# Summing over 16 ranks with identity matmuls on TensorE in place of trees on VectorE, in a two-block decoder layer pair

## The chip, the cores and the metric

One core of a Trainium2 chip runs the whole program; seven others are idle. The metric is device time in microseconds (us) of one execution.

## The reference

Two transformer blocks run one after the other on 512 tokens of width 1024. The change lies in the routing of the first block's expert layer, which reads, cut to what matters:

```python
def peer_layer(h, w_q, keys, u, v):
    q = (h @ w_q).reshape(B, S, 8, 2, 128)
    sc = jnp.einsum('bshpd,phnd->bshpn', q, keys)
    v1, i1 = lax.top_k(sc[..., 0, :], 16)
    v2, i2 = lax.top_k(sc[..., 1, :], 16)
    cand = (v1[..., :, None] + v2[..., None, :])       # 16 x 16 sums of each head
    cidx = (i1[..., :, None] * 128 + i2[..., None, :])
    best, pos = lax.top_k(cand, 16)
    idx = jnp.take_along_axis(cidx, pos, axis=-1)      # the two keys of each of the 16 best
    gates = jax.nn.softmax(best, axis=-1)
    # then act = gelu(u[idx] . h), out = sum(gates * act * v[idx])
```

Of the 256 candidates of a head only 50 can be among the best 16: rank r of the first half pairs with the first 16 // (r + 1) ranks of the second.

## The kernel before

The order on each engine is written out by hand (`manual_schedule`): an engine runs its instructions in the order in which the code issues them, and waits in place for what the next one needs. Generators that `yield` estimated microseconds are woven: `weave(main, fill, per)` lets `main` run to its next yield and then takes one step of `fill` for each `per` microseconds yielded.

The expert layer has these stages here, one after the other:

- Scoring: queries and key scores on TensorE, and the top 16 of each half on VectorE.
- Decode, `decode(tt)` for four tiles of 128 tokens. VectorE forms the 50 candidates of 8 heads (`cand`), takes their best 16 (`top16`: MAX8, MATCH_REPLACE8, FIND_INDEX8) and then turns each position `pos` into two keys. For that it compares the position with the first position of each of the 16 rows (`ge` against `row_at`), multiplies the 0/1 result by the steps between neighbouring ranks' keys (`step1`, `sum1`), and adds over the 16 ranks with a tree of four additions (L895). The row's length times 1024 rides in the same sum and is taken apart with integer operations (L898 to L904). The column in the row is then looked up the same way (L914 to L919). `turn_slots` and `keep` transpose the keys and gates of the tile before (three L942 matmuls, two ScalarE copies, four VectorE operations).
- The gate build, `gate_build`: 48 chunks, in each a comparison `hot` and a product `ohG` on VectorE, and 24 small bf16 matmuls on TensorE (L1004), evacuated by ScalarE (`gst`, L1006) and written to DRAM.
- The expert stream over 128 groups of rows of u and v.

The work woven into decode and gate build is `u_stream`. One column `a` is 24 matmuls of 128x384 (`ps_o`, L105 to L107) over a granule of u that ScalarE and GpSimd (for a < 26, `FC`) or VectorE (from 26) split into `whi` and `wlo`; a GELU (`act`, L729) ends it. A column of the first 40 is four steps of six matmuls. `early` holds the first 161 steps: decode takes one per yielded microsecond (`PER_B`), gate build one per 1.5 (`PER_C`), and what is left is issued after the gate build, before the expert stream's first v matmul (L105 to L107 with `wh`, `wl`).

Of the kernel before, what the change touches and what calls it, by code (L numbers as in the profile page):

```python
# [11 lines left out]
F32 = mybir.dt.float32  # L12
F32R = mybir.dt.float32r
BF = mybir.dt.bfloat16
I32 = mybir.dt.int32
U32 = mybir.dt.uint32
AF = mybir.ActivationFunctionType
OP = mybir.AluOpType
# [607 lines left out]
PH, PK, TOPK = 8, 128, 16  # L626
LENS = [TOPK // (i + 1) for i in range(TOPK)]
# [23 lines left out]
def top16(K, pool, work, n, tag):  # L651

    nc = K.nc
    rest = [pool.tile([128, n], F32, name="rest_" + tag, bufs=len(work)) for _ in work]
    for vals, idx, src in work:
        nc.vector.max(out=vals[:, 0:8], in_=src)
    for (vals, idx, src), r in zip(work, rest):
        nc.vector.match_replace(out=r, in_to_replace=vals[:, 0:8], in_values=src, imm_value=-3.0e38)
    for vals, idx, src in work:
        nc.vector.max_index(out=idx[:, 0:8], in_max=vals[:, 0:8], in_values=src)  # L660
    for (vals, idx, src), r in zip(work, rest):
        nc.vector.max(out=vals[:, 8:16], in_=r)
    for (vals, idx, src), r in zip(work, rest):
        nc.vector.max_index(out=idx[:, 8:16], in_max=vals[:, 8:16], in_values=r)


def peer(K, mh, w_out):
    with ExitStack() as ctx:
        ctx.enter_context(K.tc.manual_schedule())
        return peer_body(K, mh, w_out, ctx)  # L670


def peer_body(K, mh, w_out, ctx):
    nc, tc, A = K.nc, K.tc, K.A
    K.psum(ctx, mm=4, tp=2, o=2)
    P = ctx.enter_context(tc.tile_pool(name="peer", bufs=1))
    idx0 = P.tile([128, PH * TOPK], I32, name="idx0")
# [59 lines left out]
    h = mh  # L737
    with ExitStack() as c0:
        R = c0.enter_context(tc.tile_pool(name="h2", bufs=1, reuse_waits="tile"))
# [39 lines left out]
        for tt in (3, 0):  # L779
# [4 lines left out]
            for half in range(2):  # L784
                p = K.bank()
# [14 lines left out]
    with tc.tile_pool(name="route", bufs=1, reuse_waits="tile") as R:  # L800
        keys = K.xp.tile([128, 16, 128], F32, name="keys", tag="x1")
        nc.sync.dma_start(keys, A["peer_keys"])

        sh3, shk = [128, PH, TOPK], [128, TOPK, TOPK, PH]
        lens = R.tile([128, TOPK], F32, name="lens")
        row_at = R.tile(shk, BF, name="row_at")
        rank_at = R.tile(shk, BF, name="rank_at")
        for i in range(TOPK):
            nc.gpsimd.memset(row_at[:, i], float(OFFS[i]))
            nc.gpsimd.memset(lens[:, i:i + 1], 1024.0 * LENS[i - 1] if i else 0.0)  # L810
            nc.gpsimd.memset(rank_at[:, 8 * (i % 2) + 4 * (i // 2 % 2) + i // 4], float(i))
        If = R.tile([128, 2, PH, TOPK + 1], F32, name="If")
        nc.gpsimd.memset(If, 0.0)
        V = R.tile([128, NT, 2, PH, TOPK], F32, name="V")
# [10 lines left out]
        for c in range(NQ + 2):  # L825
            if c < NQ:
                pj[c] = K.proj_f(next(next_q), h)
            if 1 <= c <= NQ:
                p = K.bank("tp")
# [22 lines left out]
        RB = bctx.enter_context(tc.tile_pool(name="decode", bufs=1, reuse_waits="tile"))  # L852
        def decode(tt):

            nc.vector.tensor_copy(If[:, :, :, 1:], I[:, tt])
            v1, v2 = V[:, tt, 0], V[:, tt, 1]
            cand = RB.tile([128, PH, NCAND], F32, name="cand")
            for i in range(8):
                n = LENS[i]
                nc.vector.tensor_tensor(cand[:, :, OFFS[i]:OFFS[i] + n], v2[:, :, :n],  # L860
                                        v1[:, :, i:i + 1].to_broadcast([128, PH, n]), op=OP.add)
            nc.vector.tensor_tensor(cand[:, :, OFFS[8]:], v1[:, :, 8:],
                                    v2[:, :, 0:1].to_broadcast([128, PH, 8]), op=OP.add)
            yield 2.0
            best = RB.tile(sh3, F32, name="best")
            pos = RB.tile(sh3, U32, name="pos")
            for h0 in range(0, PH, 4):
                top16(K, RB, [(best[:, hh], pos[:, hh], cand[:, hh]) for hh in range(h0, h0 + 4)], NCAND, "c")
                yield 2.6
                if late and h0 == 0:  # L870
                    turn_slots()
                elif late:
                    keep()
                    yield 0.7

            e = RB.tile(sh3, F32, name="e")
            nc.vector.tensor_tensor(e, best, best[:, :, 0:1].to_broadcast(sh3), op=OP.subtract)
            kh = [128, TOPK, PH]
            at = RB.tile(kh, BF, name="at")
            nc.vector.tensor_copy(at, pos.rearrange("p h k -> p k h"))  # L880

            step1 = RB.tile(kh, F32, name="step1")
            nc.vector.tensor_tensor(step1, If[:, 0, :, 1:].rearrange("p h r -> p r h"),
                                    If[:, 0, :, :TOPK].rearrange("p h r -> p r h"), op=OP.subtract)
            nc.vector.tensor_tensor(step1, step1, lens[:, :, None].to_broadcast(kh), op=OP.add)
            ge = RB.tile(shk, BF, name="ge")
            nc.vector.tensor_tensor(ge, at[:, None].to_broadcast(shk), row_at, op=OP.is_ge)
            yield 2.2
            nc.scalar.activation(e, e, AF.Exp)
            sum1 = RB.tile(shk, F32, name="sum1")  # L890
            nc.vector.tensor_tensor(sum1, ge, step1[:, :, None].to_broadcast(shk), op=OP.mult)
            yield 2.2
            pk = sum1[:, 0]
            for n in (8, 4, 2, 1):
                nc.vector.tensor_tensor(sum1[:, :n], sum1[:, :n], sum1[:, n:2 * n], op=OP.add)  # L895
            yield 2.2
            pki = RB.tile(kh, I32, name="pki")
            nc.vector.tensor_copy(pki, pk)  # L898
            oi = RB.tile(kh, I32, name="oi")
            nc.vector.tensor_scalar(oi, pki, 10, None, op0=OP.arith_shift_right)  # L900
            nc.vector.tensor_scalar(pki, pki, 1023, None, op0=OP.bitwise_and)
            i1 = RB.tile(kh, F32, name="i1")
            i2 = RB.tile(kh, F32, name="i2")
            nc.vector.tensor_copy(i1, pki)  # L904
            nc.vector.tensor_tensor(at, at, oi, op=OP.subtract)
            yield 0.8

            step2 = RB.tile(kh, BF, name="step2")
            for d in range(2):
                def ranks(first):  # L910
                    return If[:, 1, :, first + d:first + d + TOPK - 1:2].rearrange("p h (q c) -> p h q c", c=2)
                nc.vector.tensor_tensor(step2[:, 8 * d:8 * d + 8].rearrange("p (c q) h -> p h q c", c=2),
                                        ranks(1), ranks(0), op=OP.subtract)
            nc.vector.tensor_tensor(ge, at[:, None].to_broadcast(shk), rank_at, op=OP.is_ge)  # L914
            yield 1.5
            nc.vector.tensor_tensor(ge, ge, step2[:, :, None].to_broadcast(shk), op=OP.mult)
            yield 1.1
            for n in (8, 4, 2, 1):
                nc.vector.tensor_tensor(ge[:, :n] if n > 1 else i2[:, None], ge[:, :n], ge[:, n:2 * n], op=OP.add)  # L919
            yield 1.3  # L920
            gs = RB.tile([128, PH], F32, name="gs")
            nc.vector.tensor_reduce(gs, e, axis=AX.X, op=OP.add)
            nc.vector.reciprocal(gs, gs)
            gt = gate0 if tt == 0 else RB.tile([128, PH * TOPK], F32, name="gt")
            g3 = gt.rearrange("p (k h) -> p h k", h=PH)
            nc.vector.tensor_tensor(g3, e, gs[:, :, None].to_broadcast(sh3), op=OP.mult)
            if tt == 0:
                nc.vector.scalar_tensor_tensor(idx0.rearrange("p (k h) -> p k h", h=PH), i1, float(PK), i2,
                                               op0=OP.mult, op1=OP.add)
                yield 1.0  # L930
                return
            yield 1.0
            late.append((i1, i2, gt, tt - 1))

# [2 lines left out]
        def turn_slots():  # L937

            i1, i2, gt, d = late.pop()
            p = K.bank("tp")  # L940
            for j, src in enumerate((i1.rearrange("p k h -> p (k h)"), i2.rearrange("p k h -> p (k h)"), gt)):
                nc.tensor.transpose(p[:, j * 128:(j + 1) * 128], src, K.ident)  # L942
            late.append((p[:, :384].rearrange("p (j c t) -> p c j t", j=3, t=OT), d))

# [12 lines left out]
        for tt in range(NT):  # L957
            weave(decode(tt), early, PER_B)
        turn_slots()
        keep()  # L960
        bctx.close()
# [115 lines left out]
    first = first_tile()  # L1077
# [18 lines left out]
    for a in range(-1, PK):  # L1096
        n = a + 1
# [852 lines left out]
```

## Time and profile before

| | us |
|---|---|
| median of three runs | 2105.06 (2104.98 to 2109.21) |
| the profiled execution | 2105.86 |
| its span, first to last instruction | 2103.60 |
| TensorE busy | 1985.4 (94%) |
| VectorE busy | 1596.6 (76%) |
| ScalarE busy | 891.1 (42%) |
| GpSimd busy | 479.2 (23%) |

A busy share is a mean over stages with different limits, so the stage around the change has to be looked at by itself. The 2.26 us between the span and the execution's time lie outside the instructions.

### The profile page before, as it was taken

How to read it: one execution, taken by the hardware profiler on the slowest of the kernel's cores; microseconds unless marked ns; L12 is line 12 of the kernel's file. 1: busy time of each engine (PE TensorE's matmuls, PEld its weight loads, DVE VectorE, ACT ScalarE, POOL GpSimd, SP SyncE). 2: the span in 40 equal slices, each digit the busy share in tenths (PEclk: the TensorE clock that was granted, in tenths of full speed). 3: DMA queues.
4: the chain of work that ended last, by engine and by line, in shares of the span. 5: the costliest groups of instructions: out<-in, count | busy, mean ns of one | idle time of the engine just before them, and what ended most of it. 6: DMA issues, size and time to landing. Idle time of an engine off the chain costs nothing.

```text
span 2103.6 us, 29961 instructions
## 1 busy us (share of the span) xinstructions
PE 1985.4 (94%) x11184; PEld 1675.0 (80%) x11184; DVE 1596.6 (76%) x3209; ACT 891.1 (42%) x1391; POOL 479.2 (23%) x395
## 2 busy tenths in 40 slices
PE   8989899999777888999999999999999999998998
PEld 6767777888777878999999999999988876666665
DVE  4557875479999996877777778878878776656677
ACT  4454433333324776333333333333334453445544
POOL 1000002200442000444444444545422001001000
PEclk9999999999988999999999999999999999999999
DMA  4214443532222557999999999999888771211111
GB/s 157 76 59 141 135 142 98 195 112 71 81 91 96 215 210 258 321 328 321 321 323 312 332 316 328 324 311 325 313 290 291 267 237 63 81 32 61 41 61 70
DMA packets 154375, 410.47 MB, mean 195 GB/s; under 512 B 13789, under 2 KB 63733, under 8 KB 150774
## 3 DMA queue, kind: packets, MB, share of 16 engines
q1 hardware_dynamic: 113332, 247.07, 34.8%
q0 software_dynamic: 37440, 136.33, 18.8%
q10 hardware_dynamic: 3458, 25.17, 3.2%
q8 instruction: 87, 1.43, 0.3%
q14 instruction: 58, 0.48, 0.1%
HBM read 378.64 MB, written 29.37 MB: 194 GB/s over the span
## 4 chain that ended last, share of the span: by engine, by line
PE 75%; DVE 15%; ACT 4%; DMA 3%; issue 2%; POOL 1%; ACTq 0%; DVEq 0%; POOLq 0%
PE ps_mm L105 12%; PE ps_mm L106 12%; PE ps_mm L107 12%; PE ps_o L105 7%; PE ps_o L107 7%; PE ps_o L106 7%; PE ps_tp L107 3%; PE ps_tp L105 3%; PE ps_tp L106 3%; PE ps_mm L1004 3%; DMA raw<-in_ada_w_dram 2%; DVE wlo L69 2%; PE ps_sc L1377 1%; PE ps_o L1362 1%; DVE sum L895 1%
## 5 line engine op out<-in xcount | busy, mean ns | idle before, releaser
L68 ACT ACTIVATE whi<-raw 128x1024 fp32r<-128x1024 f32 (+1 forms) x363 | 382.4, 1056 | 654.8 <-issue 454.6
L69 DVE TENSOR_TENSOR wlo<-raw,whi 128x1024 fp32r<-128x1024 f32 (+1 forms) x339 | 414.5, 1225 | 172.4 <-ACT whi L68 172.0
L105 PE MATMUL ps_o<-hT_hi,whi 128*128 128x384 f32 x992 | 342.4, 345 | 12.7 <-ACT act L729 12.7
L107 PE MATMUL ps_o<-hT_hi,wlo 128*128 128x384 f32 x992 | 336.8, 340 | 0.1
L106 PE MATMUL ps_o<-hT_lo,whi 128*128 128x384 f32 x992 | 335.8, 339 | 0.0
L1036 POOL DMA_INDIRECT gath<-in_peer_u_dram,idx x128 | 181.2, 1416 | 375.5 <-DVE junk L1044 185.0
L1036 POOL DMA_INDIRECT gath<-in_peer_v_dram,idx x128 | 175.8, 1373 | 257.2 <-DVE acc L1051 210.3
L105 PE MATMUL ps_mm<-hT_hi,whi 128*128 128x512 f32 (+1 forms) x544 | 224.2, 413 | 0.0
L107 PE MATMUL ps_mm<-hT_hi,wlo 128*128 128x512 f32 (+1 forms) x544 | 214.7, 395 | 0.0
L106 PE MATMUL ps_mm<-hT_lo,whi 128*128 128x512 f32 (+1 forms) x544 | 214.0, 393 | 0.0
L105 PEld LDWEIGHTS ps_o<-hT_hi,whi 128*128 128x128 f32 x992 | 189.6, 191 | 16.6 <-ACT act L729 13.3
L105 PE MATMUL ps_mm<-whi,wh 128*128 128x512 f32 x512 | 200.2, 391 | 2.0 <-ACT wh L68 2.0
L107 PE MATMUL ps_mm<-whi,wl 128*128 128x512 f32 x512 | 201.8, 394 | 0.0
L106 PE MATMUL ps_mm<-wlo,wh 128*128 128x512 f32 x512 | 201.3, 393 | 0.3 <-DVE wlo L69 0.3
L106 PEld LDWEIGHTS ps_o<-hT_lo,whi 128*128 128x128 f32 x992 | 189.4, 191 | 3.3
L107 PEld LDWEIGHTS ps_o<-hT_hi,wlo 128*128 128x128 f32 x992 | 188.8, 190 | 1.2 <-POOL wlo L69 0.8
L1051 DVE SCALAR_TENSOR_TENSOR acc<-gath,w,acc 128x1024 f32<-128x1024 f32 x127 | 162.9, 1282 | 10.7 <-DMA gath<-in_peer_v_dram,idx 8.6
L1044 DVE SCALAR_TENSOR_TENSOR junk<-gath,h 128x1024 bf16<-128x1024 f32 x128 | 156.6, 1224 | 8.9 <-DMA gath<-in_peer_u_dram,idx 6.4
L105 PEld LDWEIGHTS ps_mm<-hT_hi,whi 128*128 128x128 f32 (+1 forms) x544 | 102.9, 189 | 26.8 <-issue 6.9
L1006 ACT ACTIVATE gst<-ps_mm 128x512 f32<-128x512 f32 x96 | 104.1, 1124 | 40.1 <-PE ps_mm L1004 39.9
L107 PEld LDWEIGHTS ps_mm<-hT_hi,wlo 128*128 128x128 f32 (+1 forms) x544 | 102.5, 188 | 23.2
L106 PEld LDWEIGHTS ps_mm<-hT_lo,whi 128*128 128x128 f32 (+1 forms) x544 | 103.2, 190 | 19.2 <-DVE hT_lo L69 0.2
(477 smaller groups left out, 3502.6 us busy)
## 6 DMA issues: line engine op xcount, KB each, us to landing
raw<-in_peer_uT_dram SPq DMA_DIRECT2D x128, 512.0 KB, 5.5
raw<-in_peer_v_dram SPq DMA_DIRECT2D x128, 512.0 KB, 6.3
raw<-in_w_in_dram SPq DMA_DIRECT2D x59, 512.0 KB, 3.6
gates_dram<-gst ACTq DMA_DIRECT2D x24, 1024.0 KB, 6.9
x<-gates_dram SPq DMA_DIRECT2D x32, 768.0 KB, 9.1
raw<-in_ada_w_dram SPq DMA_DIRECT2D x24, 512.0 KB, 3.9
raw<-in_w_out_dram SPq DMA_DIRECT2D x24, 512.0 KB, 3.4
raw<-in_w_peer_q_dram SPq DMA_DIRECT2D x16, 512.0 KB, 3.7
```

The source lines that it names most:

```text
L68: self.nc.scalar.activation(hi, src, AF.Copy)
L69: (engine or self.nc.vector).tensor_tensor(lo, src, hi.bitcast(F32), op=OP.subtract)
L105: mm(out, a[0], b[0], start=start, stop=False)
L106: mm(out, a[0], b[1], start=False, stop=False)
L107: mm(out, a[1], b[0], start=False, stop=stop)
L895: nc.vector.tensor_tensor(sum1[:, :n], sum1[:, :n], sum1[:, n:2 * n], op=OP.add)
L1004: nc.tensor.matmul(ps_, hot[:, 1, t // 2, :, t % 2], Ag[:, i, t // 2, :, t % 2], start=i == 0, stop=i == 2)
L1006: nc.scalar.activation(st[:, :, t0:t0 + 4].rearrange("p a t -> p t a"), p.rearrange("p (t a) -> p t a", t=4), AF.Copy)
L1036: nc.gpsimd.indirect_dma_start(out=gath[i], out_offset=None, in_=A["peer_u" if i < NG // 2 else "peer_v"], in_offset=bass.IndirectOffsetOn ...
L1044: nc.vector.scalar_tensor_tensor(junk, g, 1.0, h0, op0=OP.mult, op1=OP.mult, accum_out=act0[:, k:k + 1])
L1051: nc.vector.scalar_tensor_tensor(acc0, g, w0[:, k:k + 1], acc0, op0=OP.mult, op1=OP.add)
L1362: nc.tensor.matmul(self.p[i * 64:(i + 1) * 64, cols], v, pt, start=i not in self.begun, stop=stop, tile_position=(0, i * 64))
```

## The change

The tree additions over ranks become matmuls. The stationary operand is the identity in bf16 (`identb`) or a multiple of it (`times[n]`, made once by ScalarE), the moving operand one rank's 128x128 slice, and 15 or 16 such matmuls add up in one third of a PSUM bank: the row's offset (`row`), the first key (`key1`) and the second key (`key2`). The product with the steps is bf16 now (`part`), and the row's length no longer rides in the key's sum, so that the integer operations go. ScalarE copies both keys out of PSUM. The yields of a tile add up to fewer microseconds. The first tile's indices `idx0`, which the gathers of the expert stream use, are formed one tile later, in `turn_slots`.

```diff
+        times = {1: K.identb}
+        for n in sorted(set(LENS) - {1}):
+            times[n] = R.tile([128, 128], BF, name=f"times{n}")
+            nc.scalar.activation(times[n], K.identb, AF.Copy, scale=float(n))
...
-            step1 = RB.tile(kh, F32, name="step1")
-            nc.vector.tensor_tensor(step1, If[:, 0, :, 1:].rearrange("p h r -> p r h"),
-                                    If[:, 0, :, :TOPK].rearrange("p h r -> p r h"), op=OP.subtract)
-            nc.vector.tensor_tensor(step1, step1, lens[:, :, None].to_broadcast(kh), op=OP.add)
+            def steps(half):
+                t = RB.tile(kh, BF, name="step", bufs=2)
+                ranks = If[:, half].rearrange("p h r -> p r h")
+                nc.vector.tensor_tensor(t, ranks[:, 1:], ranks[:, :TOPK], op=OP.subtract)
+                return t[:, :, None].to_broadcast(shk)
...
+            p = K.bank()
+            row, key1, key2 = [p[:, j * 128:(j + 1) * 128] for j in range(3)]
             ge = RB.tile(shk, BF, name="ge")
             nc.vector.tensor_tensor(ge, at[:, None].to_broadcast(shk), row_at, op=OP.is_ge)
+            step1 = steps(0)
             yield 2.2
+            for r in range(1, TOPK):
+                nc.tensor.matmul(row, times[LENS[r - 1]], flat(ge, r), start=r == 1, stop=r == TOPK - 1)
             nc.scalar.activation(e, e, AF.Exp)
-            sum1 = RB.tile(shk, F32, name="sum1")
-            nc.vector.tensor_tensor(sum1, ge, step1[:, :, None].to_broadcast(shk), op=OP.mult)
+            part = RB.tile(shk, BF, name="part")
+            nc.vector.tensor_tensor(part, ge, step1, op=OP.mult)
+            step2 = steps(1)
             yield 2.2
-            pk = sum1[:, 0]
-            for n in (8, 4, 2, 1):
-                nc.vector.tensor_tensor(sum1[:, :n], sum1[:, :n], sum1[:, n:2 * n], op=OP.add)
-            yield 2.2
-            pki = RB.tile(kh, I32, name="pki")
-            nc.vector.tensor_copy(pki, pk)
...
-            yield 0.8
...
+            for r in range(TOPK):
+                nc.tensor.matmul(key1, K.identb, flat(part, r), start=r == 0, stop=r == TOPK - 1)
+
+            nc.vector.tensor_tensor(at, at, row.rearrange("p (k h) -> p k h", h=PH), op=OP.subtract)
             nc.vector.tensor_tensor(ge, at[:, None].to_broadcast(shk), rank_at, op=OP.is_ge)
-            yield 1.5
-            nc.vector.tensor_tensor(ge, ge, step2[:, :, None].to_broadcast(shk), op=OP.mult)
-            yield 1.1
-            for n in (8, 4, 2, 1):
-                nc.vector.tensor_tensor(ge[:, :n] if n > 1 else i2[:, None], ge[:, :n], ge[:, n:2 * n], op=OP.add)
-            yield 1.3
+            yield 1.8
+            i1 = RB.tile([128, PH * TOPK], F32, name="i1")
+            i2 = RB.tile([128, PH * TOPK], F32, name="i2")
+            nc.scalar.activation(i1, key1, AF.Copy)
+            nc.vector.tensor_tensor(ge, ge, step2, op=OP.mult)
+            yield 2.0
+            for r in range(TOPK):
+                nc.tensor.matmul(key2, K.identb, flat(ge, r), start=r == 0, stop=r == TOPK - 1)
+            nc.scalar.activation(i2, key2, AF.Copy)
```

On VectorE, the middle of decode's third tile stood like this before (`sum_5363` is `sum1`, `i_5407` is `i1`, the two `step` names are `step1` and `step2`):

```order
L887 TENSOR_TENSOR ge<-at,row_at 128x2048
L891 TENSOR_TENSOR sum_5363<-ge,step_5337 128x2048
L895 TENSOR_TENSOR sum_5363<-sum_5363 128x1024
L895 TENSOR_TENSOR sum_5363<-sum_5363 128x512
L895 TENSOR_TENSOR sum_5363<-sum_5363 128x256
L895 TENSOR_TENSOR sum_5363<-sum_5363 128x128
L898 CAST pki<-sum_5363 128x128
L900 TENSOR_SCALAR oi<-pki 128x128
L901 TENSOR_SCALAR pki<-pki 128x128
L904 CAST i_5407<-pki 128x128
L905 TENSOR_TENSOR at<-at,oi 128x128
```

The same stretch stands like this in the changed kernel, from the comparison to the gate:

```order
L895 TENSOR_TENSOR ge<-at,row_at 128x2048
L885 TENSOR_TENSOR step<-If 128x128
L902 TENSOR_TENSOR part<-ge,step 128x2048
L885 TENSOR_TENSOR step<-If 128x128
L908 TENSOR_TENSOR at<-at,ps_mm 128x128
L909 TENSOR_TENSOR ge<-at,rank_at 128x2048
L914 TENSOR_TENSOR ge<-ge,step 128x2048
L920 TENSOR_REDUCE gs<-e 128x8
L921 RECIPROCAL gs<-gs 128x8
L924 TENSOR_TENSOR gt<-e,gs 128x8x16
```

The trees and the integer operations are gone, and L908 reads what TensorE summed in PSUM (`ps_mm`). On TensorE the row sum of the first tile now begins like this, between u matmuls (`times_3571` is `times[16]`, `times_3569` is `times[8]`):

```order
L105 MATMUL ps_o<-hT_hi,whi 128x384
L106 MATMUL ps_o<-hT_lo,whi 128x384
L107 MATMUL ps_o<-hT_hi,wlo 128x384
L899 LDWEIGHTS times_3571
L899 MATMUL ps_mm<-ge,times_3571 128x128
L899 LDWEIGHTS times_3569
L899 MATMUL ps_mm<-ge,times_3569 128x128
```

Before, TensorE had only u matmuls and the three transposes there. In each tile the changed order holds 15 matmuls of `row`, 12 u matmuls, 16 of `key1`, 24 u matmuls and 16 of `key2`. From one tile's first `row` matmul to the next tile's there are 96, 102 and 102 u matmuls, and from the last tile's to its transposes 42. The second key's matmuls wait for ScalarE's copy of the first, and that copy for L908, since all three sums share a bank.

After the gate build ScalarE went on like this before, from the last gates that it writes out to the first v granule (`whi_8008`); each `act` ends one u column:

```order
L1011 DMA gates_dram<-gst_7733 128x2048 x2
L68 ACTIVATE whi_7890<-raw_7752 128x1024
L729 ACTIVATE act_7921<-ps_o_7754 128x384
L68 ACTIVATE whi_7923<-raw_7894 128x1024
L729 ACTIVATE act_7954<-ps_o_7896 128x384
L68 ACTIVATE whi_7956<-raw_7927 128x1024
L729 ACTIVATE act_7987<-ps_o_7929 128x384
L68 ACTIVATE whi_8008<-raw_8002 128x1024
```

In the changed kernel it has three columns more there:

```order
L1007 DMA gates_dram<-gst_7765 128x2048 x2
L729 ACTIVATE act_7949<-ps_o_7786 128x384
L68 ACTIVATE whi_7951<-raw_7905 128x1024
L729 ACTIVATE act_7982<-ps_o_7907 128x384
L68 ACTIVATE whi_7984<-raw_7955 128x1024
L729 ACTIVATE act_8015<-ps_o_7957 128x384
L68 ACTIVATE whi_8021<-raw_7988 128x1024
L729 ACTIVATE act_8052<-ps_o_7990 128x384
L68 ACTIVATE whi_8054<-raw_8025 128x1024
L729 ACTIVATE act_8085<-ps_o_8027 128x384
L68 ACTIVATE whi_8087<-raw_8058 128x1024
L729 ACTIVATE act_8118<-ps_o_8060 128x384
```

On TensorE, the u matmuls between the last gate matmul and the first v matmul go from 96 to 162, those in the gate build from 372 to 378, and those issued ahead of the gate build are 72 fewer.

## Rows read from the trace of the kernel before

**Rows 1.** Windows: length; PE, PEld, DVE, ACT, POOL busy (instructions); PEclk, DMA share, GB/s.
```profile
532.50:658.50 126.00, 92.02 (x467) 88.36 (x467) 122.11 (x426) 39.85 (x56) 55.65 (x20) 0.86 0.27 84
658.50:820.00 161.50, 142.61 (x1545) 129.77 (x1544) 158.32 (x112) 119.65 (x127) 2.42 (x1) 1.00 0.54 196
...
839.20:1500.00 660.80, 660.46 (x3327) 600.41 (x3328) 527.38 (x666) 234.89 (x323) 309.17 (x215) 1.00 0.92 322
```

**Rows 2.** The two longest waits of TensorE, 520 to 660 us: total, times, longest.
```profile
PE ps_tp L942 <- DVE i L919: 14.5, 3, 5.5
PE ps_o L105 <- ACT act L729: 12.7, 2, 8.4
```

**Rows 3.** VectorE's timeline, decode's third tile and the gate build's beginning.
```profile
596.41 0.28 DVE L855 CAST If<-I 128x256 f32<-128x256 uint32 x1
...
605.36 0.39 DVE L883 TENSOR_TENSOR step<-If 128x128 f32<-128x128 f32 x1
...
606.00 1.22 DVE L887 TENSOR_TENSOR ge<-at,row_at 128x2048 bf16<-128x2048 bf16 x1
607.25 4.36 DVE L891 TENSOR_TENSOR sum<-ge,step 128x2048 f32<-128x2048 bf16 x1
611.64 6.99 DVE L895 TENSOR_TENSOR sum<-sum 128x1024 f32<-128x1024 f32 x4
...
622.20 1.43 DVE L914 TENSOR_TENSOR ge<-at,rank_at 128x2048 bf16<-128x2048 bf16 x1
623.67 1.23 DVE L916 TENSOR_TENSOR ge<-ge,step 128x2048 bf16<-128x2048 bf16 x1
...
626.65 0.28 DVE L922 TENSOR_REDUCE gs<-e 128x8 f32<-128x128 f32 x1
...
627.43 0.28 DVE L855 CAST If<-I 128x256 f32<-128x256 uint32 x1
...
661.48 3.42 DVE L978 TENSOR_TENSOR hot<-iota_e,ikT 128x2048 bf16<-128x2048 bf16 x1
```

**Rows 4.** GpSimd's timeline: one split in decode, one in the gate build.
```profile
606.63 2.83 POOL L69 TENSOR_TENSOR wlo<-raw,whi 128x1024 fp32r<-128x1024 f32 x1 [2.38 <-ACT whi L68]
...
661.40 2.42 POOL L69 TENSOR_TENSOR wlo<-raw,whi 128x1024 fp32r<-128x1024 f32 x1 [11.72 <-ACT whi L68]
```

**Rows 5.** TensorE's timeline: after an idle stretch, later, and a transpose.
```profile
597.55 0.52 PE L107 MATMUL ps_o<-hT_hi,wlo 128*128 128x384 f32 x1
597.87 0.52 PE L105 MATMUL ps_o<-hT_hi,whi 128*128 128x384 f32 x1
...
613.16 0.33 PE L105 MATMUL ps_o<-hT_hi,whi 128*128 128x384 f32 x1
613.33 0.33 PE L106 MATMUL ps_o<-hT_lo,whi 128*128 128x384 f32 x1
...
621.91 0.30 PE L942 MATMUL ps_tp<-ident,i 128*128 128x128 f32 x1 [1.82 <-DVE i L904]
```

**Rows 6.** The chain that ended last: start us, us, what.
```profile
545.12 1.15 DVE ge L887
...
656.92 0.32 PE ps_o L105
...
658.64 1.15 DVE hot L978
```

**Rows 7.** TensorE's timeline from the last gate matmuls to the first v matmul.
```profile
818.51 1.55 PE L1004 MATMUL ps_mm<-ohG,hot 128*128 128x128 bf16 x24 [1.12 <-ACT gst L1006]
819.87 0.42 PE L105 MATMUL ps_o<-hT_hi,whi 128*128 128x384 f32 x1
...
839.16 0.50 PE L105 MATMUL ps_mm<-whi,wh 128*128 128x512 f32 x1 [2.01 <-ACT wh L68]
```

**Rows 8.** ScalarE's timeline: the first v granule.
```profile
837.64 1.06 ACT L68 ACTIVATE whi<-raw 128x1024 fp32r<-128x1024 f32 x1 [8.28 <-DMA raw<-in_peer_v_dram]
```

**Rows 9.** The page's part 5: splits on VectorE (count, busy us, mean ns, idle).
```profile
L69 DVE TENSOR_TENSOR wlo<-raw,whi 128x1024 fp32r<-128x1024 f32 (+1 forms) x339 | 414.5, 1225 | 172.4 <-ACT whi L68 172.0
```

More of the change, by code (lines that the diff above doesn't have):

```diff
@@ L804, in peer_body @@
         sh3, shk = [128, PH, TOPK], [128, TOPK, TOPK, PH]
-        lens = R.tile([128, TOPK], F32, name="lens")
         row_at = R.tile(shk, BF, name="row_at")
@@ L809, in peer_body @@
             nc.gpsimd.memset(row_at[:, i], float(OFFS[i]))
-            nc.gpsimd.memset(lens[:, i:i + 1], 1024.0 * LENS[i - 1] if i else 0.0)
-            nc.gpsimd.memset(rank_at[:, 8 * (i % 2) + 4 * (i // 2 % 2) + i // 4], float(i))
+            nc.gpsimd.memset(rank_at[:, i], float(i))
+        times = {1: K.identb}
+        for n in sorted(set(LENS) - {1}):
+            times[n] = R.tile([128, 128], BF, name=f"times{n}")
+            nc.scalar.activation(times[n], K.identb, AF.Copy, scale=float(n))
         If = R.tile([128, 2, PH, TOPK + 1], F32, name="If")
@@ L886, in decode, with flat @@
+            def flat(t, r):
+                return t[:, r].rearrange("p k h -> p (k h)")
+            p = K.bank()
+            row, key1, key2 = [p[:, j * 128:(j + 1) * 128] for j in range(3)]
             ge = RB.tile(shk, BF, name="ge")
             nc.vector.tensor_tensor(ge, at[:, None].to_broadcast(shk), row_at, op=OP.is_ge)
+            step1 = steps(0)
             yield 2.2
+            for r in range(1, TOPK):
+                nc.tensor.matmul(row, times[LENS[r - 1]], flat(ge, r), start=r == 1, stop=r == TOPK - 1)
@@ L896, in decode @@
-            yield 2.2
-            pki = RB.tile(kh, I32, name="pki")
-            nc.vector.tensor_copy(pki, pk)
[L899 to L905, printed above, removed]
@@ L906, in decode @@
-            yield 0.8
[L908 to L913, printed above, removed]
-            nc.vector.tensor_tensor(ge, at[:, None].to_broadcast(shk), rank_at, op=OP.is_ge)
@@ L926, in decode @@
             nc.vector.tensor_tensor(g3, e, gs[:, :, None].to_broadcast(sh3), op=OP.mult)
[L927 to L931, printed above, removed]
             yield 1.0
@@ L939, in turn_slots @@
             i1, i2, gt, d = late.pop()
+            if d < 0:
+                nc.vector.scalar_tensor_tensor(idx0, i1, float(PK), i2, op0=OP.mult, op1=OP.add)
+                return
             p = K.bank("tp")
-            for j, src in enumerate((i1.rearrange("p k h -> p (k h)"), i2.rearrange("p k h -> p (k h)"), gt)):
+            for j, src in enumerate((i1, i2, gt)):
                 nc.tensor.transpose(p[:, j * 128:(j + 1) * 128], src, K.ident)
```

## The prediction

> **What bounds the kernel now.** I read the windows first, cut at the stage borders. The three windows of [rows 1] are decode, the gate build and the first part of the expert stream; the columns to compare are busy TensorE, busy VectorE and the clock. In decode VectorE is busy 122.1 of 126.0 us and TensorE 92.0, at a mean granted clock of 0.86, a mixture of its two levels 1.2 and 2.4 GHz. In the gate build VectorE is busy 158.3 of 161.5 us and the clock is full. In the expert stream TensorE is busy 660.5 of 660.8 us. So VectorE bounds decode and the gate build, and TensorE what follows: time won in decode moves the whole rest forward, and u matmuls that leave decode have to be paid where TensorE is full.
>
> The waits come next: TensorE's longest in decode are for VectorE's last tree (14.5 us) and for ScalarE's GELU (12.7 us), which stands behind an exponential that waits for VectorE [rows 2]. Then VectorE's timeline of one tile [rows 3]: from one `If` copy to the next it takes 31.0 us (596.41 to 627.43). The four f32 additions take 7.0 us of it and the f32 product 4.36. A bf16 product of the same 2048 elements takes 1.23. Much of this is not work: GpSimd's split started at 606.63 [rows 4] while the product of 607.25 had still to begin, and in the gate build a comparison of as many elements as that of 606.00 (1.22) took 3.42 from 661.48, next to a split of 661.40 to 663.82. I read that as one of the two engines waiting out the other's whole instruction, 2.2 us here.
>
> The Trainium skill says the same (SBUF — State Buffer, section Who interferes with whom): a VectorE instruction with two SBUF inputs and a GpSimd instruction that reads SBUF exclude each other for the whole instruction. The trace agrees, with 3.42 against 1.22. By that rule the new subtraction, one input of which is in PSUM, would not be held up; no row shows that.
>
> **VectorE's work per tile.** Without GpSimd's interference the changed tile is: `If` to the steps as before, 8.95 us (596.41 to 605.36); `ge` 1.25; two steps of 0.39; `part` 1.23, the price of the bf16 product; the subtraction 0.39, by the nearest row of 128x128 elements; the second comparison 1.43; its product 1.23; gate sum and gate 0.78 (626.65 to 627.43). The sum is 16.0 us against 31.0 [rows 3].
>
> **TensorE's work per tile.** A u matmul follows the one before by 0.173 us at full clock and by 0.32 at half [rows 5]. The same kind of small matmul, 128x128 bf16 with a stationary operand of its own each time, is in the gate build: 24 in 1.36 us (818.51 to 819.87), 0.057 each [rows 7]. So 47 of them cost 2.7 us a tile, and three transposes of 0.30 [rows 5] 0.9. With 102 u matmuls (17.6 us) a tile is 21.2 us of TensorE, more than VectorE's 16.0. The bound of decode passes from VectorE to TensorE, if the waits between them stay small.
>
> The Trainium skill has a dearer price (TensorE: Matmul & The Clock Gate, section Back-to-back issue gap): about 81 ns per matmul of 128 columns in a stream of weight loads and matmuls. By it the 188 new ones would cost 4.5 us more and the forecast would be 2092.5; the rows above have the duration in this kernel, so the sum goes by them.
>
> **The new waits.** TensorE now stops three times in a tile where VectorE is late, with all u matmuls behind it. Before `key1` TensorE has 0.9 us of `row` and 12 u matmuls (2.1), 3.0 in all, while VectorE needs 0.39 + 1.23 = 1.6; with one split of 2.4 us [rows 4] in between it needs 4.0, and TensorE waits 1.0. Before `key2` TensorE has 24 u matmuls, 4.2 us; VectorE needs 0.39 + 1.43 + 1.23 = 3.05, 5.45 with a split, a wait of 1.3. A split runs for more than half of a column (2.4 of 24 x 0.173 = 4.2 us), so about one of the two is hit in full: I take 1.4 us a tile, between 0 and 4.8 (two splits in full). Before `row` VectorE has some 5 us in hand (21.2 against 16.0). ScalarE's two copies and GELUs hide behind the u matmuls; what is queued behind the copy of `key1` is the next column's `whi`, needed one column later.
>
> **The sum.** From the first tile's comparison to the first `hot` it is 113.5 us now (545.12 to 658.64) [rows 6]. Changed: the first to second tile 96 u matmuls (16.6) + 2.7 + 1.4 + 2.2 = 22.9, where the 2.2 is about 15 u matmuls at half clock (15 x 0.147), as after the idle stretch of [rows 5], since in the first tile TensorE still waits several microseconds for VectorE; two tiles of 21.2 + 1.4 = 22.6; and the last 1.25 (its `ge`) + 42 u matmuls (7.3) + 2.7 + 1.4 + 0.9 + 1.7 (end of the transposes to `hot`, 656.92 to 658.64) = 15.2. Together 83.3, so 30.2 are won, and 0.64 more because `ge` now stands ahead of the steps (605.36 to 606.00) [rows 3]: 30.8 us.
>
> Two terms give back. The gate build now begins three columns earlier in u, so three more splits fall to GpSimd in a stage that VectorE bounds: 3 x 2.2 = 6.6. Two fewer fall to VectorE, 2 x 1.22 = 2.4 [rows 9]. That is 4.2 lost, between 0 (GpSimd finds gaps) and 6.6. The 6 extra u matmuls there (1.0 us) fit in TensorE's 19 idle microseconds [rows 1].
>
> The tail between the last gate matmul and the first v matmul is 19.3 us now (819.87 to 839.16) with 96 u matmuls [rows 7]. These are 16.6 us; the rest is the first v granule's transfer, for which ScalarE waited until 837.64 [rows 8]. With 162 u matmuls it is 28.0 us and the transfer is hidden: 8.7 lost, between 8.7 and 11.4 (66 x 0.173, if the transfer is late by as much as now).
>
> The setup costs nothing: six ScalarE multiples of the identity stand where TensorE is full and the next weights are a column away; uncovered they would be about 1.8 us, six of 0.30. GpSimd has 16 memsets fewer.
>
> 30.8 - 4.2 - 8.7 = 17.9. The profiled execution took 2105.86 us, 2.26 more than its span and 0.8 more than the median, so **2088.0**.
>
> **Rivals.** First, the waits (the case on the other side). Each tile has three places where TensorE stops, 12 in all. If VectorE were late by a whole split of 2.4 us at each, that is 28.8 instead of 5.6, and the time 2111.2, slower. It decides at (5.6 + 17.9) / 12 = 1.96 us a place. For it speaks that every one of these VectorE instructions has two inputs and that [rows 4] shows splits of over 2.4 us; against it the 5 us in hand before `row`, and that splits follow u columns, so that a waiting TensorE also stops them.
>
> Second, TensorE's clock. If it stayed at 1.2 GHz through decode, because the small matmuls are spread with waits, 342 u matmuls from the first `row` on would cost 0.147 more, 50 us, of which 2.2 are counted, and the time would be 2136. It decides at 122 u matmuls. For it speaks the clock of 0.86 now; against it the gate build, with the same small matmuls and many short waits at a full clock [rows 1].
>
> Third, no waits and no interference: 5.6 and 4.2 are saved, 2.4 more are VectorE's fewer splits, and the time is 2075.8.
>
> **How the numbers follow.** The forecast case holds 0.79. It spans the third rival's end, 2076, and at the other waits of 4.8 a tile (13.6 more), 2101.6; I take 2101. Waits beyond that hold 0.13, most of it between 2101 and 2109; the slow clock 0.04; better than 2076 0.04. A difference of 0.2%, 4.2 us, is about what a measurement of this kernel can tell from none. So faster 0.85, same 0.08, slower 0.07. The range is 2076 to 2101.
>
> **What would show it.** In the changed trace: `part` at about 1.2 us, or 3.5 where a split meets it; small matmuls 0.06 apart; the first `hot` near 628 instead of 658.6; TensorE nearly full from the second tile on, clock above 0.95 there; waits of `ps_mm` matmuls for `part` and `ge` of about 6 us in all; a gate build of some 166 us with four GpSimd splits; the first v matmul near 821.5, 28 us after the gate build, with no wait for the v granule; everything after it unchanged. Wrong would make it: waits on VectorE of 2 us at each place, a half clock in decode, or a tail that is longer than its u matmuls.

## The result, and the profile after

The changed kernel takes 2081.16 us (median of 4 runs, 2080.76 to 2081.91) against 2105.55 of the kernel before on the same chip: a ratio of 0.9882, 95% interval 0.9869 to 0.9895. The forecast was 2088.0. The profiled execution took 2080.84 us with a span of 2079.0, so the two traces differ by 24.6 us. Of all executions below one is left out of the medians and ratios: one of `e9_row_first` took 2776.56 us, at a clock of 0.65.

I cut the changed trace at the same stage borders as [rows 1]: decode, the gate build, and the first 50 us from the first v matmul on.

```profile
533.50:625.50 92.00, 83.72 (x589) 81.03 (x588) 80.64 (x370) 38.10 (x58) 41.21 (x17) 0.94 0.31 94
625.50:787.00 161.50, 141.33 (x1513) 128.12 (x1513) 159.86 (x109) 117.51 (x125) 13.37 (x4) 0.99 0.53 195
819.07:869.07 50.00, 50.00 (x254) 45.54 (x254) 43.38 (x64) 19.45 (x28) 22.50 (x16) 1.00 0.90 321
```

Decode's window is 92 us long instead of 126 (each begins some 12 us ahead of the first comparison, from which the table below counts). TensorE and VectorE are now almost equally busy there (83.7 and 80.6), and the clock is 0.94 instead of 0.86. The gate build is still VectorE's.

Who waits for whom from 520 to 640 us (total, times, longest) answers to [rows 2].

```profile
DVE at L908 <- PE ps_mm L906: 9.1, 4, 5.1
...
PE ps_mm L899 <- DVE ge L895: 6.7, 1, 6.7
...
PE ps_mm L917 <- DVE ge L914: 0.7, 1, 0.7
PE ps_mm L906 <- DVE part L902: 0.5, 1, 0.5
```

TensorE waited for the trees and the GELU 27.2 us before. Now it waits once for long, in the first tile before `row`, and 1.2 us in all before the key sums.

VectorE's timeline of the first tile's beginning, of the fourth tile, and of the first two `hot`, answers to [rows 3].

```profile
545.54 1.22 DVE L895 TENSOR_TENSOR ge<-at,row_at 128x2048 bf16<-128x2048 bf16 x1
...
547.08 1.22 DVE L902 TENSOR_TENSOR part<-ge,step 128x2048 bf16<-128x2048 bf16 x1
...
609.49 1.23 DVE L895 TENSOR_TENSOR ge<-at,row_at 128x2048 bf16<-128x2048 bf16 x1
610.63 0.39 DVE L885 TENSOR_TENSOR step<-If 128x128 bf16<-128x128 f32 x1
611.06 3.29 DVE L902 TENSOR_TENSOR part<-ge,step 128x2048 bf16<-128x2048 bf16 x1
...
616.67 0.29 DVE L908 TENSOR_TENSOR at<-at,ps_mm 128x128 bf16<-128x128 bf16 x1 [2.02 <-PE ps_mm L906]
616.99 2.19 DVE L909 TENSOR_TENSOR ge<-at,rank_at 128x2048 bf16<-128x2048 bf16 x1
619.22 1.22 DVE L914 TENSOR_TENSOR ge<-ge,step 128x2048 bf16<-128x2048 bf16 x1
...
625.53 1.22 DVE L974 TENSOR_TENSOR hot<-iota_e,ikT 128x2048 bf16<-128x2048 bf16 x1
...
628.45 3.41 DVE L974 TENSOR_TENSOR hot<-iota_e,ikT 128x2048 bf16<-128x2048 bf16 x1
```

GpSimd's timeline beside it answers to [rows 4].

```profile
610.64 2.63 POOL L69 TENSOR_TENSOR wlo<-raw,whi 128x1024 fp32r<-128x1024 f32 x1 [2.14 <-ACT whi L68]
615.72 2.38 POOL L69 TENSOR_TENSOR wlo<-raw,whi 128x1024 fp32r<-128x1024 f32 x1 [2.45 <-ACT whi L68]
...
627.06 3.72 POOL L69 TENSOR_TENSOR wlo<-raw,whi 128x1024 fp32r<-128x1024 f32 x1 [2.31 <-ACT whi L68]
```

`part` took 3.29 us where the split of 610.64 ran (until 613.27), and 1.22 in the first tile without one. I call such a wait of VectorE for GpSimd's split a lock. `ge` of 616.99 ends 1.1 us after the split of 615.72 does.

TensorE's timeline, with its waits in the first three tiles, the same fourth tile and the tail's end, answers to [rows 5] and [rows 7].

```profile
546.82 1.01 PE L899 MATMUL ps_mm<-ge,times 128*128 128x128 bf16 x8 [6.69 <-DVE ge L895]
...
569.23 0.61 PE L899 MATMUL ps_mm<-ge,times 128*128 128x128 bf16 x8
...
572.86 1.05 PE L906 MATMUL ps_mm<-part,identb 128*128 128x128 bf16 x16 [0.46 <-DVE part L902]
...
599.78 1.07 PE L917 MATMUL ps_mm<-ge,identb 128*128 128x128 bf16 x16 [0.69 <-DVE ge L914]
...
612.37 0.34 PE L107 MATMUL ps_o<-hT_hi,wlo 128*128 128x384 f32 x1
612.55 0.62 PE L899 MATMUL ps_mm<-ge,times 128*128 128x128 bf16 x8
613.01 0.55 PE L899 MATMUL ps_mm<-ge,identb 128*128 128x128 bf16 x7
613.37 0.42 PE L105 MATMUL ps_o<-hT_hi,whi 128*128 128x384 f32 x1
...
615.56 1.07 PE L906 MATMUL ps_mm<-part,identb 128*128 128x128 bf16 x16
616.44 0.42 PE L105 MATMUL ps_o<-hT_hi,whi 128*128 128x384 f32 x1
...
790.90 0.42 PE L105 MATMUL ps_o<-hT_hi,whi 128*128 128x384 f32 x1
...
819.07 0.39 PE L105 MATMUL ps_mm<-whi,wh 128*128 128x512 f32 x1
```

The fourth tile's 15 `row` matmuls take 0.82 us (612.55 to 613.37) and its 16 of `key1` 0.88: 0.055 each. No idle time stands before any of them. The tail runs from 790.90 to 819.07, and the first v matmul starts without a wait.

Where the 24.6 us come from, by the starts in the two traces:

| stretch | before | after | difference | forecast |
|---|---|---|---|---|
| start to the first `ge` | 545.04 | 545.54 | +0.5 | -0.6 |
| first `ge` to first `hot` | 113.5 | 80.0 | -33.5 | -30.2 |
| first `hot` to the tail's first u matmul | 161.3 | 165.4 | +4.1 | +4.2 |
| tail, to the first v matmul | 19.3 | 28.2 | +8.9 | +8.7 |
| first v matmul to the end of the span | 1264.4 | 1259.9 | -4.5 | 0 |

### The profile page after: what moved, and what is told of

It reads as the page before. It is cut to its first block, busy times and chain, and to the rows that moved or that the text cites. A ratio compares the mean times of both kernels' runs of the same rounds, so it can differ in the third digit from the quotient of the medians.

```text
span 2079.0 us, 30276 instructions
## 1 busy us (share of the span) xinstructions
PE 1985.3 (95%) x11372; PEld 1678.7 (81%) x11372; DVE 1561.3 (75%) x3153; ACT 893.7 (43%) x1405; POOL 473.4 (23%) x379
## 4 chain that ended last, share of the span: by engine, by line
PE 78%; DVE 12%; ACT 3%; issue 2%; DMA 2%; POOL 1%; DVEq 0%; ACTq 0%; POOLq 0%
PE ps_mm L105 13%; PE ps_mm L106 12%; PE ps_mm L107 12%; PE ps_o L105 8%; PE ps_o L107 8%; PE ps_o L106 8%; PE ps_tp L107 3%; PE ps_tp L106 3%; PE ps_tp L105 3%; DMA raw<-in_ada_w_dram 2%; DVE ohG L978 2%; PE ps_mm L1000 2%; DVE wlo L69 2%; DVE hot L974 2%; PE ps_sc L1373 1%
```

## The experiments

The theories: the first is the prediction's own pricing (TensorE bounds the changed decode, VectorE has some 5 us a tile in hand, a u matmul that leaves decode is paid where TensorE is full). The second says that these reserves are smaller or the prices other.

**One half alone.** `e1_first_half` is the change with the second key's sum left as a tree on VectorE, with the change's yields.

```diff
-            for r in range(TOPK):
-                nc.tensor.matmul(key2, K.identb, flat(ge, r), start=r == 0, stop=r == TOPK - 1)
-            nc.scalar.activation(i2, key2, AF.Copy)
+            for n in (8, 4, 2, 1):
+                nc.vector.tensor_tensor(ge[:, :n] if n > 1 else i2k[:, None], ge[:, :n], ge[:, n:2 * n], op=OP.add)
```

> The changed kernel with the second key's sum back as a tree on VectorE (four additions, two step operations, no key2 matmuls, no ScalarE copy of it); same yields, so the u matmuls stand as in the changed kernel (438 in decode, 378 in the gate build, 162 after it). Theory 1, TensorE bounds the changed decode: VectorE gets 1.5 + 0.3 + 0.35 = 2.1 us more a tile and has about 5 in hand; TensorE loses 16 matmuls a tile, 0.9 us, so about 2078 us, 3.6 less than the changed kernel's 2081.2. Theory 2, VectorE's chain through the waits still sets decode: 2.1 to 4.4 us more in each of four tiles, 2090 to 2098 us.

Measured: 2101.35 us, ratio 0.9975 (0.9961 to 0.9990), slower than both theories allowed. Decode takes 97.0 us (545.78 to 642.75). The waits of this kernel from 520 to 640 us:

```profile
PE ps_mm L899 <- DVE ge L895: 20.4, 4, 6.7
...
DVE at L914 <- PE ps_mm L912: 16.3, 4, 4.5
```

Both engines wait for each other, in every tile. VectorE's timeline of the third tile:

```profile
596.82 1.23 DVE L895 TENSOR_TENSOR ge<-at,row_at 128x2048 bf16<-128x2048 bf16 x1
597.96 0.37 DVE L885 TENSOR_TENSOR step<-If 128x128 bf16<-128x128 f32 x1
598.37 1.23 DVE L902 TENSOR_TENSOR part<-ge,step 128x2048 bf16<-128x2048 bf16 x1
...
604.68 0.29 DVE L914 TENSOR_TENSOR at<-at,ps_mm 128x128 bf16<-128x128 bf16 x1 [4.46 <-PE ps_mm L912]
605.01 3.18 DVE L915 TENSOR_TENSOR ge<-at,rank_at 128x2048 bf16<-128x2048 bf16 x1
```

And TensorE's rows of it:

```profile
598.10 1.01 PE L899 MATMUL ps_mm<-ge,times 128*128 128x128 bf16 x8 [3.53 <-DVE ge L895]
598.91 0.95 PE L899 MATMUL ps_mm<-ge,identb 128*128 128x128 bf16 x7
...
603.58 1.07 PE L912 MATMUL ps_mm<-part,identb 128*128 128x128 bf16 x16
604.45 0.42 PE L105 MATMUL ps_o<-hT_hi,whi 128*128 128x384 f32 x1
```

TensorE idles for `ge`. Behind that wait it runs at 1.2 GHz (a clock of 0.51 from 598.10 to 603.58, 8 small matmuls in 0.81 us instead of 0.46), so that `row`, 12 u matmuls and `key1` take 6.4 us (598.10 to 604.45) instead of the 3.9 of the change's fourth tile (612.55 to 616.44). VectorE's subtraction needs only `row`, but stands in the code behind `key1`, which adds up in the same bank, and waits for that too. Then VectorE is late with the next `ge`. I call this a ring: each engine waits for the other. It was a new theory, tested further down (`e8_first_half_row_first`).

`e2_second_half` is the kernel before with only the second key as matmuls.

```diff
-            for n in (8, 4, 2, 1):
-                nc.vector.tensor_tensor(ge[:, :n] if n > 1 else i2[:, None], ge[:, :n], ge[:, n:2 * n], op=OP.add)
+            for r in range(TOPK):
+                nc.tensor.matmul(key2, K.identb, ge[:, r].rearrange("p k h -> p (k h)"), start=r == 0, stop=r == TOPK - 1)
+            nc.scalar.activation(i2f, key2, AF.Copy)
```

> The kernel before with only the second key's sum as 16 identity matmuls (first half with its f32 tree and integer operations as before, yields as before: 510 u matmuls in decode, 372 in the gate build, 96 after it). Both theories have VectorE as the bound here; it sheds 2.1 us a tile without GpSimd's interference (2.6 with it): 8.4 to 10.4 us, about 2096 us. If the second half were worth as much as the first, 2093.

Measured: 2102.21 us, ratio 0.9964 (0.9950 to 0.9978), 7.6 us less than before. The size is nearly the expected one, but the expected cause does not show. The windows from the first `ge` to the first `hot`, of the kernel before and of this one, and this one's longest waits on either side:

```profile
545.04:658.55 113.51, 82.37 (x411) 79.03 (x412) 109.75 (x336) 35.41 (x51) 50.67 (x18) 0.84 0.26 79
547.83:662.43 114.60, 88.09 (x487) 87.08 (x488) 93.86 (x316) 37.49 (x56) 46.66 (x18) 0.84 0.25 75
...
PE ps_mm L918 <- DVE ge L914: 25.0, 4, 7.8
...
DVE g3T L952 <- ACT ikT L950: 17.2, 3, 6.1
```

VectorE sheds 15.9 us of busy time (109.75 to 93.86), but decode is no shorter. TensorE now waits 25.0 us for the product ahead of `key2`, and VectorE 17.2 us for ScalarE's copy of the transposed keys, which come from TensorE. So VectorE alone was no longer the bound, against what both theories took for granted. This trace is of the slowest of the five executions (2106.57 us); where the faster ones gain is not shown.

**The yields alone, and the matmuls without them.** The smaller yields move 72 u matmuls out of decode. `e3_trees_new_yields` does that to the kernel before, `e4_matmuls_old_yields` undoes it in the change; both get there by `PER_B`.

```diff
-PER_B, PER_C = (1.0, 1.5)
+PER_B, PER_C = (1.185, 1.5)    # e3_trees_new_yields, on the kernel before
+PER_B, PER_C = (0.845, 1.5)    # e4_matmuls_old_yields, on the change
```

> The kernel before, trees and all, with the weave's rate in decode set to 1.185 in place of 1.0, so that the u matmuls stand exactly as in the changed kernel (438 in decode, 378, 162). Theory 1, the gain comes from taking the trees off VectorE and the moved columns are a loss: decode stays at 113.5 us from the first comparison to the first one-hot, the gate build is 4 us longer, the tail 9, and the first v matmuls run 2.6 faster: about 2116 us. Theory 3, the gain comes from the smaller share of u work in decode: decode shrinks and the time falls below 2100.

Measured: 2114.93 us, ratio 1.0036 (1.0023 to 1.0048). The tail is 28.2 us, and decode still takes 112.5 (543.82 to 656.30): where trees bound it, fewer u matmuls win little (1.0 us) and are paid later.

> The changed kernel with the weave's rate in decode set to 0.845, so that the u matmuls stand as before the change (510 in decode, 372, 96). Theory 1, TensorE bounds the changed decode: 72 u matmuls more there are 12.5 us more, the gate build is 4 shorter, the tail 9 shorter, and the first v matmuls run at half clock again (2.6): about 2083 us, within 3 of the changed kernel. Theory 2, VectorE's chain sets decode: decode is no longer, the other terms stay, about 2071 us.

Measured: 2079.15 us, ratio 0.9861 (0.9847 to 0.9876). Decode is 89.4 us, 9.4 more than in the change, the gate build 161.3 and the tail 18.4.

```profile
546.66:636.04 89.38, 86.97 (x610) 84.77 (x610) 79.12 (x282) 38.71 (x60) 42.53 (x18) 0.96 0.32 98
```

Of the 72 u matmuls 60 stand in this stretch, 10.4 us at 0.173; the other 12 stand ahead of it, where TensorE's wait before the first `row` shrinks from 6.7 to 4.7 us. So decode grows nearly by what TensorE gets more, as theory 1 has it. The half clock at the first v matmuls did not come (a clock of 1.00 over the first 50 us). The matmuls are thus worth 1.4% (with the old yields) to 1.55% (with the new, 0.988 / 1.0036). The new yields cost the kernel before 0.36%. In the change it is 0.2%, which the intervals alone can't tell from none; by the traces the three stages together are 4.5 us longer with the new yields (273.5 against 269.0).

**What gives back.** The next four ran side by side on another chip: the change unaltered, smaller yields in the gate build (`PER_C`), three columns fewer for GpSimd (`FC`), and both.

```diff
-FC = 26
+FC = 23                        # e6_fc23, e7_both
-PER_B, PER_C = (1.0, 1.5)
+PER_B, PER_C = (1.0, 1.3)      # e5_per_c, e7_both
```

> The changed kernel again, unaltered, beside the three runs that follow on the same chip. All theories: a ratio of 0.988 to the kernel before.

Measured: 2082.12 us, ratio 0.9880 (0.9864 to 0.9895).

> The changed kernel with the weave's rate in the gate build at 1.3 in place of 1.5: 438 u matmuls there in place of 378, and 102 after it in place of 162. Theory 1, VectorE bounds the gate build and leaves TensorE some 20 us there, while the tail is TensorE's: the gate build is no longer, the tail falls from 28.2 to the 19 us that the first v granule's transfer takes, and 2.6 us of half clock come back at the first v matmuls: 6 us less than the changed kernel, a ratio of 0.985. Rival, the gate build stretches by the 10.4 us of u matmuls that it takes in, and nothing is gained: 0.988 or more.

Measured: 2077.47 us, ratio 0.9855 (0.9840 to 0.9870). The gate build takes 167.6 us (2.3 more), the tail 18.5 (9.7 less): the 60 u matmuls fit for the most part into TensorE's idle time of the gate build, as the prediction said of six. No half clock came back at the first v matmuls (254 matmuls in 50 us, as in the change).

> The changed kernel with GpSimd splitting u only up to column 22 in place of 25, so that the gate build's splits are all VectorE's. Theory 1, GpSimd's split locks VectorE out for 2.2 us each: the one-hot comparisons of 3.4 us in the gate build's start become 1.2, three VectorE splits of 1.2 are added, and the gate build is 3 us shorter (ratio 0.9868). Rival, the 4 us by which the gate build grew have another cause: no shorter, 0.988 or, with VectorE's added splits, 0.990.

Measured: 2078.50 us, ratio 0.9869 (0.9854 to 0.9884). The gate build takes 162.4 us instead of 165.4, 3.0 less; three splits at 2.2 minus three at 1.22 on VectorE are 2.9. One product in the changed kernel's gate build, next to GpSimd's split of 650.59:

```profile
651.66 3.83 DVE L978 TENSOR_TENSOR ohG<-hot,g3T 128x3072 bf16<-128x3072 bf16 x1
```

The same product in this kernel, where VectorE does the split:

```profile
650.78 1.76 DVE L978 TENSOR_TENSOR ohG<-hot,g3T 128x3072 bf16<-128x3072 bf16 x1
```

> Both of the two edits before (rate 1.3 in the gate build, GpSimd's splits up to column 22). Theory 1, they add: 9 us less than the changed kernel, a ratio of 0.984. If the gate build has no room for VectorE's added splits together with more u columns, no better than the better of the two.

Measured: 2071.84 us, ratio 0.9826 (0.9812 to 0.9840), better than both kernels by some 10 and 36 us. The two add: the gate build takes 164.6 us and the tail 19.7, together 9.2 less than in the change (184.3 and 193.5).

**The ring.** The subtraction that reads `row`, and the comparison behind it, are issued ahead of `key1` in the code. The order on every engine stays the same; VectorE waits for `row` alone. It is done to `e1_first_half`, to the change (`e9_row_first`) and to `e7_both` (`e10_both_row_first`).

```diff
+            nc.vector.tensor_tensor(at, at, row.rearrange("p (k h) -> p k h", h=PH), op=OP.subtract)
+            nc.vector.tensor_tensor(ge, at[:, None].to_broadcast(shk), rank_at, op=OP.is_ge)
             yield 2.2
             for r in range(TOPK):
                 nc.tensor.matmul(key1, K.identb, flat(part, r), start=r == 0, stop=r == TOPK - 1)
-            nc.vector.tensor_tensor(at, at, row.rearrange("p (k h) -> p k h", h=PH), op=OP.subtract)
-            nc.vector.tensor_tensor(ge, at[:, None].to_broadcast(shk), rank_at, op=OP.is_ge)
```

> The first experiment (second key by a tree) with one thing moved: the subtraction that reads the row sum, and the comparison behind it, stand ahead of the first key's matmuls in the code. The order on every engine stays the same; only VectorE no longer waits for the first key's sum before it subtracts. In the first experiment VectorE waited for that sum 16.3 us in all (4 times) and TensorE for ge 20.4 us (4 times). Theory A (the two engines wait for each other in a ring, and VectorE's wait for the first key is the part of it that is not work): VectorE's tile falls from 25.5 us towards 21.4, TensorE's own work is 20.4; three tiles win 3.5 to 4 us and the first some, so 2085 to 2090, ratio 0.990 to 0.992. Theory B (VectorE is simply full there, by its trees and by GpSimd's locks): the wait is slack that turns up elsewhere, and the time stays above 2097, ratio 0.995 or more.

Measured: 2086.5 us, ratio 0.9896 (0.9879 to 0.9913): theory A. VectorE's third tile, now without a wait:

```profile
588.99 1.23 DVE L895 TENSOR_TENSOR ge<-at,row_at 128x2048 bf16<-128x2048 bf16 x1
590.13 2.57 DVE L885 TENSOR_TENSOR step<-If 128x128 bf16<-128x128 f32 x1
592.74 1.23 DVE L902 TENSOR_TENSOR part<-ge,step 128x2048 bf16<-128x2048 bf16 x1
...
594.21 0.50 DVE L910 TENSOR_TENSOR at<-at,ps_mm 128x128 bf16<-128x128 bf16 x1
```

TensorE's waits for `ge` fall from 20.4 us to 9.2 (two times), and decode from 97.0 to 80.0 us (548.05 to 627.96), as long as in the change although VectorE still adds the second key. GpSimd's locks are still there (2.57 for a step, 3.28 for the next comparison), and VectorE's busy time in decode falls by only 1.7 us (78.0 to 76.3). So 15.3 of the 17.0 us were waits, not work or locks. Half of the gain falls to the first tile (25.5 to 17.0 us), to which the expectation gave only "some": 4.4 us are the wait, and 4.2 two locks that its tree no longer meets, while other tiles meet more. Whether a bank of its own for each sum would open the ring as well was not tried.

> The change with the same move. There VectorE waited for the first key's sum 9.1 us in all, but TensorE waited for VectorE only once for long (6.7 us before the first row sum, which the move cannot reach). Theory A and B alike: TensorE bounds decode, so VectorE's earlier subtraction gives it nothing but the two waits of 0.5 and 0.7 us; 2080 to 2082 beside 2081 to 2082 of the change, ratio 0.987 to 0.988. More than 4 us better would mean that TensorE did not bound the changed decode.

Measured: 2081.96 us (three executions), ratio 0.9872 (0.9853 to 0.9892). Decode is 78.1 us (547.0 to 625.1) instead of 80.0, and the time can't be told from that of the change: TensorE is the bound there, as both theories said. Beside `e8_first_half_row_first` it is 4.5 us faster, with overlapping intervals: once `row` is read early, the second key's matmuls are worth little here.

> The version with smaller yields in the gate build and three columns fewer for GpSimd, with the same move. Expected as that version, 2071 to 2072, ratio 0.9826 (0.981 to 0.984); it is run as a candidate for the best one.

Measured: 2071.07 us, ratio 0.9822 (0.9805 to 0.9839): with `e7_both` the best version, and not to be told from it.

## Why the prediction was right, and where it was off

**The direction and the mechanism** held. Decode's bound passed from VectorE to TensorE, `part` took 1.22 or 3.3 us, the small matmuls stood 0.055 apart and the clock was 1.00 from the second tile's `row` on. `e4_matmuls_old_yields` shows the matmuls alone to be worth the whole gain, and `e9_row_first` that VectorE no longer sets the changed decode. The half clock came where it was forecast, behind the first tile's wait of 6.7 us: 12 u matmuls stood 0.32 apart there, with 31 small ones around them, and from 553.70 on the pace was 0.17. Up to the end of `key1` that took 6.6 us (546.82 to 553.45) instead of 3.9, so it cost 2.7 us, not 2.2; the forecast had left the small matmuls out.

**The waits** were the term mis-sized inside decode: "I take 1.4 us a tile", 5.6 us in all, and the trace has 1.2 (0.5 before `key1`, 0.7 before `key2`). The number of hits was right: of the eight key sums four had a split in full ahead of them (before `key1` in the second to fourth tiles, before `key2` in the third) and one in part. Their price was wrong. The forecast took `row` to begin when `ge` ends, and a hit to cost the whole split of 2.4 us. But `ge` ended at 569.19, 589.84 and 610.72 in the second to fourth tiles, and `row` began at 569.23, 590.76 and 612.55, in the last two behind u matmuls. So VectorE had 0.0, 0.9 and 1.8 us in hand there. In the fourth tile the lock of `part` (done at 614.35) was over before `key1` began at 615.56; only in the second, with nothing in hand, did TensorE wait for `part`, and 0.5 us instead of 1.0, since the lock added 2.1 (3.30 instead of 1.23). From one `row` to the next in the second to fourth tiles TensorE needed 21.7 us on average (569.23 to 590.76 to 612.55), not 22.6, and from the last `row` to `hot` 13.0, not 14.0. With 0.5 less in the first tile that is the 3.3 us that decode came out better. TensorE's own 21.2 us a tile were right (21.1 without the waits), though the three transposes took 0.24 of them and not 0.9.

**"Before `row` VectorE has some 5 us in hand"** was wrong in kind. It compared two sums of work, 21.2 and 16.0, and left out that VectorE waits for TensorE in each tile: 9.1 us in all, of which the first tile has 5.1. What it had in hand at `row` was 0.0 to 1.8 us, as above. `e1_first_half` puts 2.1 us a tile more on VectorE, by its expectation, which is more than that, and falls into the ring; `e8_first_half_row_first` opens the ring and gets 17.0 us of decode back. In the change the ring is only not closed. As a side result, most of what the second half of the change seems worth (`e1_first_half` against the change, some 20 us) is the price of the order in which `row` and `key1` are read.

**The gate build** (+4.1 for 4.2) and **the tail** (+8.9 for 8.7) came as reckoned. `e6_fc23` confirms the price of a split, 2.2 us of VectorE, to a tenth. ScalarE's `whi` of the first v granule still waited 5.0 us for its transfer in the changed kernel, at 816.45, but that ended before TensorE needed it: hidden, as forecast.

**The start** gained what was forecast, but run-to-run differences hide it. From the transpose of `mod_acc` near 335 us, ahead of every changed instruction, to the first `ge` it is 211.4 us before and 210.6 after (0.6 forecast). The other traces have the same two values, with the tree for the first key and without it. But that transpose itself came 1.3 us later in the profiled run after (333.68 and 334.98), and anywhere from 332.46 (`e3_trees_new_yields`) to 339.03 (`e5_per_c`) in others.

**"Everything after it unchanged"** was the second step that failed, for about 3 us. In [rows 7] TensorE waits 2.01 us for `wh`, and in the 50 us that follow the kernel before has this window:

```profile
839.16:889.16 50.00, 49.66 (x239) 44.21 (x240) 42.11 (x61) 20.34 (x28) 23.49 (x16) 0.97 0.93 324
```

There are 239 matmuls at a clock of 0.97, where the changed kernel has 254 at 1.00. Fifteen matmuls at 0.2 us (50 / 254) are 3 us, an estimate from these two windows. The longer tail took away the wait in front of the v matmuls, and the lower clock behind it did not come. The other 1.5 of the 4.5 us are not shown to come from the change: `c_after`, the same kernel with 253 matmuls in those 50 us, took 1263.4 us from its first v matmul on instead of 1259.9, and over all traces that stretch ranges from 1259.4 (`e6_fc23`) to 1265.4 (`e8_first_half_row_first`).

**The rivals**: waits at 12 places (2111) did not come, since VectorE was ahead; a half clock through decode (2136) did not come; no waits and no interference (2075.8) had the waits nearly right (1.2 us) and the interference wrong. The dearer price for the small matmuls, by which the prediction gives 2092.5, did not come either: 0.055 each.

## What to carry to other kernels

When work passes from one engine to another, don't compare two sums of work alone: follow one round of the ring between them, with the position in the queue at which each waits, and see which result each wait really needs. A read that stands in the code behind a later sum in the same accumulator bank can tie a consumer to more than it reads; moving that read cost the change nothing (`e9_row_first`) and won 17 us of decode where the ring was closed. Where other work is woven in by yields, set the yields again after such a change, in the stage that has idle time on the engine in question: here that, with a fairer share between GpSimd and VectorE, gave 10 us more.

## What the runs showed of the hardware

- VectorE's subtraction with one input in PSUM (`at`, L908) took 0.29 us at 616.67, inside GpSimd's split of 615.72 to 618.10, while the comparison right behind it, with both inputs in SBUF, took 2.19 instead of 1.22. Each of the ten traces with this subtraction has one that ran inside a split in 0.29 us. This is what the prediction said that no row showed. The Trainium skill (SBUF — State Buffer, section Who interferes with whom) names two SBUF inputs as the condition, and the trace agrees.
- A wait right ahead of the first v matmul can go with a fall of TensorE's clock to 1.2 GHz behind it, but need not. The windows of the first 50 us, of `e7_both` (wait 1.03 us) and of `e4_matmuls_old_yields` (wait 1.07):

```profile
812.31:862.31 50.00, 49.66 (x239) 44.23 (x240) 42.12 (x61) 20.34 (x28) 23.20 (x16) 0.97 0.91 322
815.71:865.71 50.00, 49.66 (x248) 44.69 (x249) 42.67 (x62) 20.50 (x28) 24.14 (x16) 1.00 0.91 331
```

  With 2.01 us in the kernel before and 2.18 in `e2_second_half` it fell too (239 matmuls each); without a wait, in the change and in `e5_per_c` and `e10_both_row_first`, it did not (254).
- TensorE's small matmuls with a stationary operand each cost 0.055 us at full clock (16 in 0.88) and 0.1 at half (8 in 0.81).
